# Sliding-window attention: the product of probabilities and reciprocal sums computed on GpSimd instead of the Vector engine

## The chip, the cores and the metric

The kernel runs on one core of a Trainium2 chip. The core's engines are named as the profile names them: PE (TensorE, the matrix products; PEld is its loading of stationary operands), DVE (VectorE), ACT (ScalarE), POOL (GpSimd) and SP (SyncE, which issues most loads). Each runs its own instructions in a fixed order and waits on semaphores for the others. The metric is the device time of one launch in microseconds; before the change it is 1203.77 us, the median of three runs from 1203.2 to 1205.82.

## The reference

A two-layer decoder trunk over 512 tokens of width 1024: an mLSTM layer, then a sliding-window attention layer with sinks, each followed by a layer norm, a squared-ReLU MLP, a second norm and a gated embedding. The change is in the attention of the second layer, where each of 16 heads sees a window of 128 tokens:

```python
scores = jnp.where(valid[None, :, None, None], scores, -jnp.inf)
...
m = jnp.maximum(jnp.max(scores, axis=-1), sink)
e = jnp.exp(scores - m[..., None])
probs = e / (jnp.sum(e, axis=-1) + jnp.exp(sink - m))[..., None]
out = jnp.einsum('bnqkgs,bnskd->bnqkgd', probs.astype(x.dtype), vb).reshape(B, S, D_MODEL)
```

## The kernel before

All products are made in three parts (`mm3`, lines 87 to 90): every float32 operand is split into a rounded high part and the low rest, and PE adds high by high, high by low and low by high. The split costs an ACT copy (the high part) and a DVE subtraction (the low part), for weights in `load_w` (lines 76 and 77) and for every intermediate result.

The attention layer is cut into 16 blocks, named (g, t) here: g is one of four groups of four heads that share a key and value head, t one of four tiles of 128 tokens. `q_group(g, t)` makes the queries of a block (24 products of 256 columns into the bank `mm`, a DVE sum `q` at line 839 that frees the bank, rotation on POOL at lines 786 to 789, transposes, split). `attend(g, t)` does the attention of a block, in this chain:

- PE: eight score products (lines 860 and 861) into two `sc` banks.
- DVE: masked copy (865), maximum (866), then the negative maximum `anm` (871) and the sink term `es` (873).
- ACT: four exponentials (879), which write the probabilities `pr` (128 x 512) and their sums `sm`.
- DVE: sum with the sink (881), reciprocal (882), and the product of `pr` and the reciprocal, spread over 128 columns per head (883).
- PE: four transposes of `pr` (887) into a `pt` bank.
- ACT copies the high part `ah` (891), DVE subtracts for the low part `al` (892).
- POOL, for t > 0: two triangular selects make `bh` and `bl` (899).
- PE: six value products with `ah` and `al`, and six more with `bh` and `bl` (the masked products), at lines 88 to 90 on tiles `pt`. ACT (910) and DVE (911) split the result into `QS`.

The program issues `attend(g, ...)` for four tiles and then `q_group(g + 1, ...)`, so the query products of the next group are the work that covers the chain; in the last group the first products of the output projection (`wo_part`, 128 x 512 into `mm`) take that part. `pr`, `ah`, `al`, `bh` and `bl` have two buffers each, `sc` has three banks, `mm` and `pt` two.

The order in which each engine takes these instructions isn't written by hand. The framework's scheduler sets it when the program is built, from its own estimate of each instruction's duration and engine. So a change of engine for one instruction can move others, on every engine.

## Time and profile before

| what | value |
|---|---|
| median of three runs | 1203.77 us |
| the profiled execution in all | 1205.69 us |
| its span | 1204.0 us |
| granted TensorE clock over the span | 0.998 |
| first and last multiply of line 883 | 674.1 and 761.6 us |

The profile shows one execution. "Busy" is the time in which an engine has an instruction at work, "idle before" the time that it stood still ahead of one, with the instruction that ended the wait. The attention blocks fill about 90 us of the span, from 671 to 761 us; the MLP of the first layer lies before, the output projection, the norm and the second MLP behind. Rows of the timeline give start and duration in us, engine, line, operation, and the tiles written and read.

### The profile page before, as it was taken

To read this page: it belongs to the slowest core of one execution; us is meant where nothing else is said; L and a number is where in the kernel's file an instruction comes from. 1 tells how busy PE (TensorE), PEld (TensorE's weight loads), DVE (VectorE), ACT (ScalarE), POOL (GpSimd) and SP (SyncE) were. 2 spreads that over 40 slices of the span, in tenths; PEclk is the share of its full clock that TensorE was granted. 3 is DMA by queue.
4 is the path that set the end of the run, shared out by engine and by line. 5 is a ranking of instruction groups with operands and counts; after the bars stand their busy time and mean duration, and the time that the engine had idled before them with its cause. 6 is when DMAs were issued, how large, how long until landed. Compare 5 with 4: busy or idle time off the path is not lost. (4 is left out here: it accounts for less than half of the span.)

```text
span 1204.0 us, 15649 instructions
## 1 busy us (share of the span) xinstructions
PE 1178.7 (98%) x5918; PEld 1001.0 (83%) x5918; DVE 879.0 (73%) x1451; ACT 587.5 (49%) x1016; POOL 95.8 (8%) x189
## 2 busy tenths in 40 slices
PE   8999999999999999999999999989999999999998
PEld 7899998888888888888788998779888888888877
DVE  6555556878488589599786888596847848959974
ACT  4645552565464463464344655346645536346431
POOL 1011020100000000001201342110000000000100
PEclk9999999999999999999999999999999999999999
DMA  7322226214505306215252211361350440631511
GB/s 247 101 80 69 84 89 260 90 35 128 153 1 175 105 19 194 68 53 160 76 180 101 71 37 36 122 228 36 94 169 18 140 141 1 191 89 36 155 56 52
DMA packets 35707, 124.54 MB, mean 103 GB/s; under 512 B 4064, under 2 KB 4592, under 8 KB 35632
## 3 DMA queue, kind: packets, MB, share of 16 engines
q1 hardware_dynamic: 33552, 116.46, 30.4%
q0 software_dynamic: 2080, 7.09, 1.8%
q8 instruction: 46, 0.75, 0.2%
q14 instruction: 29, 0.24, 0.1%
HBM read 119.34 MB, written 4.19 MB: 103 GB/s over the span
## 5 line engine op out<-in xcount | busy, mean ns | idle before, releaser
L77 DVE TENSOR_TENSOR wlo<-wraw,whi 128x1024 fp32r<-128x1024 f32 (+1 forms) x168 | 204.1, 1218 | 125.2 <-ACT whi L76 124.2
L76 ACT CAST whi<-wraw 128x1024 fp32r<-128x1024 f32 (+1 forms) x168 | 173.7, 1037 | 239.6 <-PE mm L90 132.8
L88 PE MATMUL mm<-XH,whi 128*128 128x512 f32 (+1 forms) x640 | 235.1, 370 | 1.2 <-ACT ot L230 1.0
L89 PE MATMUL mm<-XL,whi 128*128 128x512 f32 (+1 forms) x640 | 235.9, 369 | 0.0
L90 PE MATMUL mm<-XH,wlo 128*128 128x512 f32 (+1 forms) x640 | 235.7, 369 | 0.0
L88 PE MATMUL mm<-whi,XH 128*128 128x512 f32 (+2 forms) x424 | 146.0, 345 | 3.9 <-DVE q L839 2.2
L89 PE MATMUL mm<-wlo,XH 128*128 128x512 f32 (+2 forms) x424 | 145.3, 343 | 0.0
L90 PE MATMUL mm<-whi,XL 128*128 128x512 f32 (+2 forms) x424 | 144.7, 343 | 0.0
L88 PEld LDWEIGHTS mm<-XH,whi 128*128 128x128 f32 x640 | 120.4, 189 | 21.8 <-ACT ot L230 1.4
L90 PEld LDWEIGHTS mm<-XH,wlo 128*128 128x128 f32 x640 | 121.1, 189 | 20.0
L89 PEld LDWEIGHTS mm<-XL,whi 128*128 128x128 f32 x640 | 121.1, 189 | 19.6
L76 ACT CAST whi<-rb 128x1024 fp32r<-128x1024 f32 x80 | 84.0, 1050 | 101.0 <-PE mm L89 56.4
L77 DVE TENSOR_TENSOR wlo<-rb,whi 128x1024 fp32r<-128x1024 f32 x80 | 97.4, 1221 | 38.9 <-ACT whi L76 38.9
L88 PEld LDWEIGHTS mm<-whi,XH 128*128 128x128 f32 x424 | 79.9, 189 | 13.0 <-DVE q L839 3.9
L89 PEld LDWEIGHTS mm<-wlo,XH 128*128 128x128 f32 x424 | 80.1, 189 | 7.7 <-issue 1.5
L90 PEld LDWEIGHTS mm<-whi,XL 128*128 128x128 f32 x424 | 80.1, 189 | 6.5 <-issue 0.8
L89 PE MATMUL mm<-wlo,S23h 128*128 128x512 f32 x128 | 50.7, 396 | 0.0
L89 PE MATMUL mm<-wlo,S4Ah 128*128 128x512 f32 x128 | 50.6, 395 | 0.0
L88 PE MATMUL mm<-whi,S23h 128*128 128x512 f32 x128 | 50.6, 395 | 0.0
L88 PE MATMUL mm<-whi,S4Ah 128*128 128x512 f32 x128 | 50.6, 395 | 0.0
L90 PE MATMUL mm<-whi,S4Al 128*128 128x512 f32 x128 | 50.3, 395 | 0.0
L633 DVE TENSOR_TENSOR res<-res,mm 128x512 f32<-128x512 f32 x72 | 48.6, 682 | 1.5 <-PE mm L90 1.0
(356 smaller groups left out, 2233.2 us busy)
## 6 DMA issues: line engine op xcount, KB each, us to landing
wraw<-in_w_up_dram SPq DMA_DIRECT2D x64, 512.0 KB, 3.9
rb<-in_w_down_dram SPq DMA_DIRECT2D x48, 512.0 KB, 4.4
wraw<-in_w_down_dram SPq DMA_DIRECT2D x16, 512.0 KB, 3.5
wraw<-in_w_gate_dram SPq DMA_DIRECT2D x16, 512.0 KB, 3.8
wraw<-in_w_vo_dram SPq DMA_DIRECT2D x19, 412.0 KB, 3.5
wraw<-in_w_qk_dram SPq DMA_DIRECT2D x8, 512.0 KB, 3.7
wraw<-in_w_out_dram SPq DMA_DIRECT2D x8, 512.0 KB, 3.9
wraw<-in_w_q_dram SPq DMA_DIRECT2D x8, 512.0 KB, 3.9
```

What stands on the lines that cost most here:

```text
L76: ACT.copy(hi, raw)
L77: eng.tensor_sub(lo, raw, f32(hi))
L88: PE.matmul(o, lh, rh, start=start, stop=False)
L89: PE.matmul(o, lh, rl, start=False, stop=False)
L90: PE.matmul(o, ll, rh, start=False, stop=stop)
L633: V.tensor_add(r[:, h], r[:, h], bank)
```

## The change

Line 883 moves from DVE (`V`) to POOL (`GP`); nothing else is edited.

```diff
         V.tensor_add(sm, sm, es)
         V.reciprocal(sm, sm)
-        V.tensor_mul(pt_, pt_, sm.unsqueeze(3).broadcast_to([P, 2, 2, P]))
+        GP.tensor_mul(pt_, pt_, sm.unsqueeze(3).broadcast_to([P, 2, 2, P]))
         pT = bank("pt")
```

The scheduler gives all four computing engines a new order from the fourth block on. Three places follow.

PE, block (1,1). `pr_6177` is its probabilities, `sc_6272` and `sc_6279` are the scores of block (1,3), `ah_6191` and `al_6192` its own split probabilities. Before, from its transposes on:

```order
L887 MATMUL pt_6186<-ident_66,pr_6177 128x128 x4
L860 MATMUL sc_6279<-KH_5264,QS_5326 128x256
L861 MATMUL sc_6279<-KL_5265,QS_5326 128x256
L860 MATMUL sc_6272<-KH_5264,QS_5326 128x256
L861 MATMUL sc_6272<-KL_5265,QS_5326 128x256
L860 MATMUL sc_6279<-KH_5264,QS_5326 128x256
L861 MATMUL sc_6279<-KL_5265,QS_5326 128x256
L843 MATMUL tp_6361<-ident_66,q_6353 128x128 x2
L88 MATMUL pt_6199<-ah_6191,vo0h_5272 128x256
L89 MATMUL pt_6199<-al_6192,vo0h_5272 128x256
```

After, from the same transposes on:

```order
L887 MATMUL pt_6186<-ident_66,pr_6177 128x128 x4
L860 MATMUL sc_6272<-KH_5264,QS_5326 128x256
L861 MATMUL sc_6272<-KL_5265,QS_5326 128x256
L843 MATMUL tp_6361<-ident_66,q_6353 128x128 x2
L860 MATMUL sc_6279<-KH_5264,QS_5326 128x256
L861 MATMUL sc_6279<-KL_5265,QS_5326 128x256
L860 MATMUL sc_6279<-KH_5264,QS_5326 128x256
L861 MATMUL sc_6279<-KL_5265,QS_5326 128x256
L88 MATMUL mm_6407<-whi_6099,XH_64 128x256
L89 MATMUL mm_6407<-wlo_6100,XH_64 128x256
```

Query products (`mm_6407`, 21 of them before the first value product of the block) now follow where the value products stood.

PE, block (2,2). `ah_6636` and `al_6637` are its split probabilities, `pr_6679` those of the next block, `mm_7021` is a bank of the output projection. Before, behind the last score products that follow its transposes:

```order
L860 MATMUL sc_6906<-KH_5264,QS_5326 128x256
L861 MATMUL sc_6906<-KL_5265,QS_5326 128x256
L88 MATMUL mm_7021<-whi_6875,QS_5326 128x512
L89 MATMUL mm_7021<-wlo_6876,QS_5326 128x512
L90 MATMUL mm_7021<-whi_6875,QS_5326 128x512
L88 MATMUL mm_7021<-whi_6875,QS_5326 128x512
```

After, at the same place:

```order
L860 MATMUL sc_6906<-KH_5264,QS_5326 128x256
L861 MATMUL sc_6906<-KL_5265,QS_5326 128x256
L88 MATMUL pt_6644<-ah_6636,vo1h_5278 128x256
L89 MATMUL pt_6644<-al_6637,vo1h_5278 128x256
L90 MATMUL pt_6644<-ah_6636,vo1l_5279 128x256
L88 MATMUL pt_6644<-ah_6636,vo1h_5278 128x256
L89 MATMUL pt_6644<-al_6637,vo1h_5278 128x256
L90 MATMUL pt_6644<-ah_6636,vo1l_5279 128x256
L88 MATMUL pt_6644<-bh_6640,vs2h_5296 128x256
L887 MATMUL pt_6688<-ident_66,pr_6679 128x128 x4
L88 MATMUL mm_7021<-whi_6875,QS_5326 128x512
```

Fourteen out-projection products stood ahead of the value products; now they stand behind them and behind the next block's transposes.

POOL and DVE, the last four blocks (3,0) to (3,3), whose probabilities are `pr_6918`, `pr_6984`, `pr_7060` and `pr_7117`. `bh_7002` and `bl_7003` belong to (3,1), `bh_7078` and `bl_7079` to (3,2). POOL before:

```order
L899 AFFINE_SELECT bh_6697<-ah_6693 128x512
L899 AFFINE_SELECT bl_6698<-al_6694 128x512
L899 AFFINE_SELECT bh_7002<-ah_6998 128x512
L899 AFFINE_SELECT bl_7003<-al_6999 128x512
L899 AFFINE_SELECT bh_7078<-ah_7074 128x512
L899 AFFINE_SELECT bl_7079<-al_7075 128x512
```

POOL after:

```order
L883 TENSOR_TENSOR pr_6918<-pr_6918,sm_6919 128x512
L883 TENSOR_TENSOR pr_6984<-pr_6984,sm_6985 128x512
L899 AFFINE_SELECT bh_7002<-ah_6998 128x512
L899 AFFINE_SELECT bl_7003<-al_6999 128x512
L883 TENSOR_TENSOR pr_7060<-pr_7060,sm_7061 128x512
L883 TENSOR_TENSOR pr_7117<-pr_7117,sm_7118 128x512
L899 AFFINE_SELECT bh_7078<-ah_7074 128x512
L899 AFFINE_SELECT bl_7079<-al_7075 128x512
```

The multiply of (3,2) stands behind both selects of (3,1), and the selects of (3,2) behind the multiply of (3,3). On DVE at the same place, `al_6933` is the low part of block (3,0), `anm_6979` the negative maximum of (3,1), `sc_7041` a score of (3,2). Before:

```order
L866 TENSOR_REDUCE smax_6964<-sc_6972 128x2
L849 TENSOR_TENSOR QS_5326<-tp_6828,QS_5326 64x2x128
L871 SCALAR_TENSOR_TENSOR anm_6979<-smax_6964,nsink_5270 128x4
L892 TENSOR_TENSOR al_6933<-pt_6927,ah_6932 128x512
L873 TENSOR_TENSOR es_6981<-sinkb_332,anm_6979 128x4
L865 COPY_PREDICATED sc_7041<-mask_328,sc_7041 128x2x128
```

After:

```order
L892 TENSOR_TENSOR al_6933<-pt_6927,ah_6932 128x512
L865 COPY_PREDICATED sc_7041<-mask_328,sc_7041 128x2x128
L849 TENSOR_TENSOR QS_5326<-tp_6867,QS_5326 64x2x128
L871 SCALAR_TENSOR_TENSOR anm_6979<-smax_6964,nsink_5270 128x4
L866 TENSOR_REDUCE smax_7040<-sc_7041 128x2
L873 TENSOR_TENSOR es_6981<-sinkb_332,anm_6979 128x4
```

The low part of (3,0) and a masked copy of (3,2) now stand ahead of the maximum of (3,1).

## Prediction

> **What bounds the kernel now.** I read the page first: busy shares, then the chain that ended last.

> ```profile
> PE 1178.7 (98%) x5918; PEld 1001.0 (83%) x5918; DVE 879.0 (73%) x1451; ACT 587.5 (49%) x1016; POOL 95.8 (8%) x189
> PE 32%; DVE 1%; ACT 0%; issue 0%
> ```

> TensorE sets the end. A change on DVE or GpSimd can only win back time in which PE waits, or add such time. So the second view is busy time by stretch, cut at the attention blocks: 671 to 749 us holds the multiplies of blocks (0,0) to (3,0), 749 to 760 the last blocks that no projection work covers, then the output projection and the first norm.

> ```profile
> core 0: us, PE busy (x) PEld busy (x) DVE busy (x) ACT busy (x) POOL busy (x), PEclk, DMA share, GB/s
> 671.00:749.00 78.00, 74.29 (x570) 69.89 (x569) 66.26 (x177) 44.95 (x173) 27.23 (x65) 1.00 0.14 44
> 749.00:760.00 11.00, 9.32 (x61) 7.59 (x60) 9.91 (x30) 6.34 (x29) 1.27 (x2) 1.00 0.00 0
> 760.00:780.00 20.00, 20.00 (x101) 16.82 (x100) 7.38 (x12) 6.17 (x15) 3.98 (x6) 1.00 0.38 133
> 780.00:812.00 32.00, 28.19 (x159) 23.72 (x158) 30.52 (x45) 13.03 (x19) 5.97 (x4) 1.00 0.67 246
> ```

> PE idles 78.00 - 74.29 = 3.7 us in the covered blocks and 11.00 - 9.32 = 1.7 us in the last ones; from 760 to 780 it does not wait. Hence 5.4 us is the whole prize, and DVE is 85 to 90% busy there. The view of waits says for whom PE waited between 671 and 762:

> ```profile
> PE mm L88 <- DVE q L839: 2.2, 4, 0.7
> PE pt L89 <- DVE al L892: 1.3, 2, 0.9
> PE pt L88 <- DVE QS L911: 0.5, 1, 0.5
> ```

> All three are late DVE work, so the idea has something to win.

> **What the multiply costs on each engine.** DVE and its nearest relatives on GpSimd:

> ```profile
> L883 DVE TENSOR_TENSOR pr<-pr,sm x16: 680/686/1008, 674.1 to 761.6; 128x512 f32<-128x512 f32 x16
> L395 POOL TENSOR_TENSOR ot<-ot,hg 128x1024 f32<-128x1024 f32 x4 | 9.6, 2403 | 44.4 <-ACT ot L394 44.4
> L786 POOL TENSOR_TENSOR ta<-q,cos 128x64 f32<-128x64 f32 x16 | 6.1, 380 | 100.5 <-DVE q L839 89.5 <-DVE es L873 7.5 <-PE pt L90 3.3
> L899 POOL TENSOR_SCALAR_AFFINE_SELECT bh<-ah 128x512 fp32r<-128x512 f32 x12 | 8.1, 676 | 40.6 <-ACT ah L891 40.6
> ```

> Removed: 16 x 0.686 = 11.0 us of DVE. Added: a two-input product of 512 columns on GpSimd, which no row shows. A line through 64 columns (380 ns) and 1024 columns (2403 ns) gives 380 + 448 x 2.11 = 1.32 us; I take that. The ends are 0.68 us (the select of the same tile, one input) and 2.40 us (twice the width). GpSimd gets 16 x 1.32 = 21 us on top of the 28.5 us in the 89 us above: room enough, if the queue's order allows it. [...]

> **Covered blocks, the waits that go.** Block (0,0):

> ```profile
> 673.43 0.18 DVE L882 RECIPROCAL sm<-sm 128x4 f32<-128x4 f32 x1
> ...
> 673.58 0.28 PE L860 MATMUL sc<-KH,QS 128*128 128x256 f32 x1
> ...
> 673.70 0.28 PE L861 MATMUL sc<-KL,QS 128*128 128x256 f32 x1
> ...
> 674.09 0.69 DVE L883 TENSOR_TENSOR pr<-pr,sm 128x512 f32<-128x512 f32 x1
> ...
> 674.82 0.43 DVE L865 COPY_PREDICATED sc<-mask,sc 128x256 f32<-128x256 uint8 x1
> 674.84 0.66 PE L887 MATMUL pt<-ident,pr 128*128 128x128 f32 x4
> ...
> 675.62 0.41 DVE L839 TENSOR_TENSOR q<-mm,bq 128x256 f32<-128x256 f32 x1
> ...
> 676.09 0.39 PE L88 MATMUL mm<-whi,XH 128*128 128x256 f32 x1 [0.59 <-DVE q L839]
> ```

> PE waits 0.59 us for the sum q (it frees the bank), and q stood behind the multiply. Without it the masked copy, whose score (673.70 + 0.28) is done, starts 0.7 us earlier, and q with it. On GpSimd the multiply can start at 673.7, not at 674.09, and ends at 675.0 against 674.78: the transposes slip by 0.2, and after their 0.5 us of issue the product can follow at 675.6 instead of 676.09. I count **-0.5**. So latency is nearly even here: what GpSimd loses in speed it gains by not queueing on DVE.

> ```profile
> 707.49 0.39 PE L89 MATMUL pt<-al,vo0h 128*128 128x256 f32 x1 [0.89 <-DVE al L892]
> ...
> 711.87 0.69 DVE L883 TENSOR_TENSOR pr<-pr,sm 128x512 f32<-128x512 f32 x1
> 712.48 1.22 DVE L77 TENSOR_TENSOR wlo<-wraw,whi 128x1024 fp32r<-128x1024 f32 x1
> 713.73 0.42 DVE L839 TENSOR_TENSOR q<-mm,bq 128x256 f32<-128x256 f32 x1
> ...
> 714.21 0.38 PE L88 MATMUL mm<-whi,XH 128*128 128x256 f32 x1 [0.67 <-DVE q L839]
> 747.62 0.36 PE L88 MATMUL pt<-ah,vo2h 128*128 128x256 f32 x1 [0.53 <-DVE QS L911]
> ```

> Block (1,1) waits 0.89 us for al. In the new PE order 21 projection products, at 0.12 us each (673.58 to 673.70), stand between its transposes and its value products: **-0.9**. At 714.21 q stood behind a multiply and a weight split; now it follows the reciprocal directly: **-0.7**. At 747.62 block (2,3) gets projection products ahead of its value products: **-0.5**. Together **-2.6**.

> **Covered blocks, a wait that comes.** The same reordering takes cover from block (2,2): its value products stood behind 15 short products and 14 of the wide out-projection ones after its transposes; now only the 15 are left, 1.8 us at 0.12.

> ```profile
> 737.41 0.60 PE L887 MATMUL pt<-ident,pr 128*128 128x128 f32 x4
> 739.95 0.68 DVE L892 TENSOR_TENSOR al<-pt,ah 128x512 fp32r<-128x512 f32 x1
> ```

> al was ready 3.2 us after the transposes began; with one multiply less ahead, 2.5 to 2.8; needed some 0.4 + 1.8 = 2.2 after: a wait of about 0.5. The first masked product of that block stands ahead of the next transposes, and its select now queues behind the next block's multiply on GpSimd: 0.6 more. **+1.1**.

> **The last blocks.** Transposes of (3,0), (3,1), (3,2), and the chain between the last two:

> ```profile
> 748.94 0.60 PE L887 MATMUL pt<-ident,pr 128*128 128x128 f32 x4
> ...
> 755.67 0.63 PE L887 MATMUL pt<-ident,pr 128*128 128x128 f32 x4 [0.32 <-DVE es L873]
> ...
> 756.50 0.59 ACT L891 CAST ah<-pt 128x512 fp32r<-128x512 f32 x1
> ...
> 757.25 0.67 DVE L892 TENSOR_TENSOR al<-pt,ah 128x512 fp32r<-128x512 f32 x1
> 757.98 0.64 POOL L899 TENSOR_SCALAR_AFFINE_SELECT bl<-al 128x512 fp32r<-128x512 f32 x1 [0.18 <-DVE al L892]
> 758.15 1.00 DVE L883 TENSOR_TENSOR pr<-pr,sm 128x512 f32<-128x512 f32 x1
> ...
> 759.37 0.60 PE L887 MATMUL pt<-ident,pr 128*128 128x128 f32 x4
> ```

> From (3,2)'s transposes on PE never waits, and the products left are the same number in both orders; so the end moves with 759.37. Select and multiply ran beside each other; in the new GpSimd order the multiply of (3,2) stands behind both selects of (3,1). The chain is then 0.63 + 0.59 + 0.67 + 0.64 + 1.32 and about 0.7 of hand-offs and queueing behind the exponentials = 4.6 us against 759.37 - 755.67 = 3.7: +0.9. Between (3,0) and (3,1) DVE now does al of (3,0) ahead of the maximum of (3,1), and the longer multiply adds to it: +0.5 on 6.7 us. Five masked products of (2,3) that filled that gap (0.6 us) are now ahead of it: +0.6. And the maximum of (3,2), with two inputs in SBUF, meets the running multiply of (3,1). What such a meeting costs:

> ```profile
> 112.27 2.40 POOL L395 TENSOR_TENSOR ot<-ot,hg 128x1024 f32<-128x1024 f32 x1 [10.88 <-ACT ot L394]
> 113.26 2.29 DVE L77 TENSOR_TENSOR wlo<-wraw,whi 128x824 fp32r<-128x824 f32 x1
> L77 DVE TENSOR_TENSOR wlo<-wraw,whi x168: 1016/1224/2289, 21.2 to 1175.2; 128x1024 fp32r<-128x1024 f32 x152, 128x824 fp32r<-128x824 f32 x16
> ```

> The split beside the GpSimd product ended 0.88 us after it: it stood still until GpSimd was done. Here that is 0 to 0.8 us; I take half: +0.4. **Together +2.4.**

> After 780 PE idles 3.8 us behind norms on DVE; the same work, slightly reordered: 0, give or take 0.5.

> **Sum:** -2.6 + 1.1 + 2.4 = **+0.9 us** on the profiled execution (1204.0 span, 1205.69 in all), 1206.6. Its three runs have a median of 1203.77, so I forecast **1204.7**. With the multiply at 0.68 us, (2,2) and the two last steps get 0.64 shorter each: -1.0; at 2.40, 1.08 longer each: +4.1.

> **Rivals.** *Relief wins.* DVE loses 11 us in a stage where it is the late one: all 3.7 us of idle PE up to 749 go, and the last blocks pay only 0.6, one longer multiply: -3.1, 1200.7. For it: all three rows of waits name DVE. Against: the reordering also spends cover, and the last blocks are a chain.

> *GpSimd's multiply becomes the chain (slower).* Place: the transposes of (2,2) to (3,2), which wait for it. Price: at 2.0 us (blocked by a split, or slower than the line) each of (2,2), (3,1), (3,2) adds 0.7, and so does (0,0), whose transposes (674.84) followed DVE's multiply at once: 0.9 + 2.8 = +3.7, 1207.5. It decides from about 1.7 us per multiply. For it: the 2.29 us row, and GpSimd's fixed order. Against: in (0,0) the earlier start pays for most of the longer multiply.

> *The two engines only trade places.* Every DVE op with two SBUF inputs stands still behind the multiply, so DVE gains nothing that PE sees, and the last blocks keep their time because the copy and split there hide it: 0, 1203.8. [...] The 2.29 us row agrees that they meet; whether it eats the gain no row shows yet.

> **How the numbers follow.** Forecast 0.46, relief 0.22, GpSimd chain 0.24, trade 0.08. About 0.2% (2.4 us) is what a measurement of this kernel can tell from no change: faster is below 1201.4, slower above 1206.2. Faster: relief less a little, plus the forecast's low end = 0.23; slower: the GpSimd chain and the forecast's high end = 0.29; same 0.48. The forecast's own range is 1202.5 to 1206.5; both signs hold half the chance, so the range takes in most of both rivals: 1200.5 to 1208.2.

> **What would show it.** GpSimd's multiply at 1.2 to 1.4 us; PE's waits for q near 675 and 714 gone; a new wait of about 1 us around block (2,2); 11 to 13 us from (3,0)'s to (3,2)'s transposes instead of 10.4; PE full for 20 us after. Wrong if the multiply is far from 1.3 us, if PE's idle time up to (3,0) does not fall below 3.7, or if the time differs outside the attention stage.

## The result, and the profile after

| | before | after |
|---|---|---|
| median of 5 runs | 1203.77 us | 1210.36 us |
| lowest to highest | 1203.1 to 1205.82 us | 1209.21 to 1211.33 us |
| the profiled execution: in all, span, mean clock | 1205.69, 1204.0 us, 0.998 | 1210.66, 1209.0 us, 0.996 |

The ratio is 1.0044, interval 1.0033 to 1.0055: the change costs about 5.3 us, with 4.0 to 6.6 us possible. (The two medians are 6.6 us apart, the upper end of this.) The forecast was 1204.7 us, with 1208.2 as its upper end.

First the multiply itself and the waits of the attention stage, 671 to 762 us, after the change (a group's row: count, shortest, median and longest in ns; a wait's row: total, times, longest in us):

```profile
L883 POOL TENSOR_TENSOR pr<-pr,sm x16: 1029/1040/1042, 673.9 to 760.8; 128x512 f32<-128x512 f32 x16
```

```profile
PE mm L88 <- DVE q L839: 1.8, 3, 0.8
PE pt L88 <- DVE al L892: 1.3, 1, 1.3
...
PE pt L887 <- POOL pr L883: 0.4, 1, 0.4
```

GpSimd needs 1.04 us for the product, and TensorE waits for it only once, 0.4 us. The waits for other engines have changed places. The stretches of the prediction, with the same columns, after the change:

```profile
671.00:749.00 78.00, 74.93 (x583) 71.26 (x584) 62.44 (x168) 46.34 (x175) 39.58 (x79) 1.00 0.15 45
749.00:760.00 11.00, 7.44 (x43) 5.55 (x41) 8.09 (x25) 6.23 (x32) 3.23 (x4) 1.00 0.00 1
760.00:780.00 20.00, 19.86 (x102) 16.83 (x103) 6.56 (x10) 5.54 (x10) 4.70 (x8) 1.00 0.32 101
780.00:812.00 32.00, 25.57 (x124) 20.55 (x123) 25.96 (x37) 11.12 (x14) 4.52 (x3) 0.95 0.67 249
```

The covered blocks got better (idle TensorE 3.1 us instead of 3.7), the last blocks worse (3.6 instead of 1.7). Up to the transposes of block (3,2), which start at 760.14 instead of 759.37, that makes +0.8 us (0.2 of it stands there before the stage begins: the same product starts at 670.82 instead of 670.62). The rest comes after 780 us: TensorE idles 32.00 - 25.57 = 6.4 us instead of 3.8, and the granted clock over these 32 us is 0.95 instead of 1.00, which is 1.6 us of full speed. 0.8 + 2.6 + 1.6 = 5.0 us, the difference of the two spans.

What stands there is one stop of TensorE (timeline of the changed kernel, TensorE, then VectorE):

```profile
786.53 0.50 PE L88 MATMUL mm<-whi,QS 128*128 128x512 f32 x1 [4.42 <-DVE res L157]
786.86 0.39 PE L89 MATMUL mm<-wlo,QS 128*128 128x512 f32 x1
787.09 0.49 PE L90 MATMUL mm<-whi,QS 128*128 128x512 f32 x1
787.38 0.63 PE L88 MATMUL mm<-whi,QS 128*128 128x512 f32 x1
787.80 0.63 PE L89 MATMUL mm<-wlo,QS 128*128 128x512 f32 x1
```

```profile
782.29 0.69 DVE L157 TENSOR_TENSOR res<-res,mm 128x512 f32<-128x512 f32 x1 [5.82 <-DMA res<-spill]
...
785.19 1.28 DVE L157 TENSOR_TENSOR res<-res,mm 128x512 f32<-128x512 f32 x2 [1.48 <-DMA res<-spill]
```

The same adds in the kernel before, and the product of TensorE that waited for the second of them:

```profile
779.87 0.69 DVE L157 TENSOR_TENSOR res<-res,mm 128x512 f32<-128x512 f32 x1 [3.71 <-DMA res<-spill]
...
781.20 0.67 DVE L157 TENSOR_TENSOR res<-res,mm 128x512 f32<-128x512 f32 x1
782.45 0.69 DVE L157 TENSOR_TENSOR res<-res,mm 128x512 f32<-128x512 f32 x1 [0.58 <-DMA res<-spill]
```

```profile
781.93 0.50 PE L88 MATMUL mm<-whi,QS 128*128 128x512 f32 x1 [0.57 <-DVE res L157]
```

Behind the attention stage the output projection is added to the residual tiles `res` (line 157), which come back from memory (`spill`, line 946) into space that the attention tiles leave. TensorE goes on 0.06 us after the add of the first tile's second half: before at 781.20 + 0.67, when it waited 0.6 us, after behind 785.19 + 1.28, when it waited 4.4. Two things delay that add. The first reload arrives 2.4 us later. And the scheduler has put the add of the second tile's first half, with its own reload, ahead of it in VectorE's queue. SyncE's issues, before and after:

```profile
771.36 2.91 SPq L83 DMA_DIRECT2D wraw<-in_w_up_dram  x3
774.37 2.09 SPq L946 DMA_DIRECT2D res<-spill  x4
```

```profile
771.95 3.12 SPq L83 DMA_DIRECT2D wraw<-in_w_up_dram  x3
775.17 2.24 SPq L946 DMA_DIRECT2D res<-spill  x4
```

The reloads are issued 0.8 us later, behind three weight loads of 512 KB each for a stage that needs them much later. They wait for nothing of their own: SyncE's longest wait there, 32.2 us before and 33.0 us after, is that of the first of these weight loads, for a buffer that a weight split (line 77) frees. Then the clock (stretches of 2 us, after):

```profile
786.00:788.00 2.00, 1.47 (x5) 1.20 (x6) 2.00 (x4) 0.00 (x0) 0.00 (x0) 0.81 1.04 418
788.00:790.00 2.00, 2.00 (x7) 1.52 (x6) 2.00 (x5) 0.00 (x0) 0.38 (x1) 0.50 1.02 418
```

Soon after TensorE starts again, its clock is halved for 3.4 us (787.25 to 790.66): products start 0.42 us apart (787.38, 787.80), 0.23 before (786.86, 787.09). The stop of 4.42 us stands ahead of it here; in the experiments below the half clock also comes behind less (2.3 us in before_late_reload).

### The profile page after: what moved, and what is told of

It reads as the page before. It is cut to its first block, busy times and chain, and to the rows that moved or that the text cites. A ratio compares the mean times of both kernels' runs of the same rounds, so it can differ in the third digit from the quotient of the medians.

```text
span 1209.0 us, 15663 instructions
## 1 busy us (share of the span) xinstructions
PE 1179.7 (98%) x5918; PEld 1002.3 (83%) x5918; DVE 873.1 (72%) x1435; ACT 587.7 (49%) x1016; POOL 110.8 (9%) x205
## 4 chain that ended last, share of the span: by engine, by line
PE 87%; DVE 6%; ACT 3%; DMA 2%; issue 1%; SPq 0%; POOL 0%; DVEq 0%; ACTq 0%; POOLq 0%
PE mm L88 28%; PE mm L90 28%; PE mm L89 27%; DVE wlo L77 1%; ACT pr L879 1%; PE tp L129 1%; DMA xraw<-in_xT_dram 1%; DMA res<-spill 1%; ACT whi L76 1%; PE tp L88 1%; PE tp L89 1%; PE tp L90 1%; DVE sc L865 1%; DVE QS L849 1%; DVE smax L866 1%
## 5 line engine op out<-in xcount | busy, mean ns | idle before, releaser
L77 DVE TENSOR_TENSOR wlo<-wraw,whi 128x1024 fp32r<-128x1024 f32 (+1 forms) x168 | 205.2, 1224 | 126.9 <-ACT whi L76 126.0
L88 PE MATMUL mm<-XH,whi 128*128 128x512 f32 (+1 forms) x640 | 235.7, 370 | 1.0 <-ACT ot L230 0.8
L90 PE MATMUL mm<-XH,wlo 128*128 128x512 f32 (+1 forms) x640 | 236.1, 369 | 0.0
L89 PE MATMUL mm<-XL,whi 128*128 128x512 f32 (+1 forms) x640 | 236.1, 369 | 0.0
L88 PE MATMUL mm<-whi,XH 128*128 128x512 f32 (+2 forms) x424 | 146.3, 346 | 3.6 <-DVE q L839 1.8
L89 PE MATMUL mm<-wlo,XH 128*128 128x512 f32 (+2 forms) x424 | 145.1, 343 | 0.0
L90 PE MATMUL mm<-whi,XL 128*128 128x512 f32 (+2 forms) x424 | 144.4, 343 | 0.0
L88 PEld LDWEIGHTS mm<-XH,whi 128*128 128x128 f32 x640 | 120.8, 190 | 21.4 <-ACT ot L230 1.2
L90 PEld LDWEIGHTS mm<-XH,wlo 128*128 128x128 f32 x640 | 121.3, 190 | 20.0
L89 PEld LDWEIGHTS mm<-XL,whi 128*128 128x128 f32 x640 | 121.3, 189 | 19.8
L77 DVE TENSOR_TENSOR wlo<-rb,whi 128x1024 fp32r<-128x1024 f32 x80 | 97.6, 1225 | 39.0 <-ACT whi L76 39.0
L88 PEld LDWEIGHTS mm<-whi,XH 128*128 128x128 f32 x424 | 79.9, 189 | 12.6 <-DVE q L839 3.4
L89 PEld LDWEIGHTS mm<-wlo,XH 128*128 128x128 f32 x424 | 80.2, 189 | 7.7 <-issue 1.5
L90 PEld LDWEIGHTS mm<-whi,XL 128*128 128x128 f32 x424 | 80.1, 189 | 6.5 <-issue 0.8
L89 PE MATMUL mm<-wlo,S23h 128*128 128x512 f32 x128 | 50.7, 396 | 0.0
L89 PE MATMUL mm<-wlo,S4Ah 128*128 128x512 f32 x128 | 50.6, 396 | 0.0
L88 PE MATMUL mm<-whi,S23h 128*128 128x512 f32 x128 | 50.6, 395 | 0.0
L88 PE MATMUL mm<-whi,S4Ah 128*128 128x512 f32 x128 | 50.6, 395 | 0.0
L90 PE MATMUL mm<-whi,S4Al 128*128 128x512 f32 x128 | 50.3, 395 | 0.0
```

The source lines that it names most:

```text
L77: eng.tensor_sub(lo, raw, f32(hi))
L88: PE.matmul(o, lh, rh, start=start, stop=False)
L89: PE.matmul(o, lh, rl, start=False, stop=False)
L90: PE.matmul(o, ll, rh, start=False, stop=stop)
```

## The experiments

Three theories were on the table. **A**: the order of the two adds. **B**: the attention stage itself, with the multiply on GpSimd. **C**: the reload that comes late, in whatever order. The kernel before was timed anew beside each group of kernels (medians 1205.03, 1204.97, 1205.00 and 1204.76 us); a ratio of 0.001 is 1.2 us. "First add" is the start of the first add of line 157, "stop" TensorE's wait for these adds, "half clock" whether the stretch behind the stop shows it, all from one profiled execution each, which can lie up to 2.7 us off its kernel's median.

| kernel | median us | ratio and interval | reload issued | first add | stop | half clock |
|---|---|---|---|---|---|---|
| before | 1203.77 | 1 | 774.37 | 779.87 | 0.6 | no |
| after | 1210.36 | 1.0044 (1.0033 to 1.0055) | 775.17 | 782.29 | 4.4 | yes |
| after_adds_as_before | 1208.41 | 1.0032 (1.0020 to 1.0043) | 774.54 | 781.45 | 2.0 | no |
| before_adds_as_after | 1205.71 | 1.0010 (1.0000 to 1.0021) | 773.68 | 779.66 | 2.6 | yes |
| gp_groups_0_2 | 1209.08 | 1.0039 (1.0026 to 1.0051) | 774.16 | 781.23 | 4.9 | yes |
| after_reload_first | 1203.46 | 0.9993 (0.9983 to 1.0002) | 767.05 | 776.09 | none | no |
| before_reload_first | 1201.52 | 0.9970 (0.9958 to 0.9981) | 765.73 | 774.79 | none | no |
| after_bc_behind | 1206.89 | 1.0010 (1.0001 to 1.0019) | 774.87 | 781.88 | 2.7 | yes |
| after_filled_stop | 1206.27 | 1.0014 (1.0005 to 1.0023) | 774.64 | 782.00 | 0.7 | no |
| gp_block_00 | 1204.74 | 0.9995 (0.9986 to 1.0005) | 772.57 | 777.80 | 0.3 | no |
| before_late_reload | 1208.29 | 1.0032 (1.0019 to 1.0046) | 776.13 | 782.36 | 2.3 | yes |
| gp_0_1_reload_first | 1199.64 | 0.9953 (0.9941 to 0.9965) | 764.11 | 773.17 | none | no |
| gp_0_2_reload_first | 1205.08 | 1.0002 (0.9993 to 1.0010) | 769.35 | 778.39 | 0.8 | no |
| gp_groups_0_1 | 1203.37 | 0.9985 (0.9976 to 0.9994) | 771.70 | 777.06 | 0.4 | no |

### after_adds_as_before: the order of the adds put back

```diff
+            if half == 0 and t == 1:
+                late = ps
+                continue
             r = add_res(t, half, ps, None)
+            if half == 1 and t == 0:
+                with tc.issue_after(tc.nc.cur_bb.bb.instructions[-1]):
+                    r1 = add_res(1, 0, late, None)
+                    V.bn_stats(sts[1][:, 0, :], r1)
```

> The changed kernel with the two adds of L157 put back in the old order: the add of (second tile, first half) is queued on VectorE behind the add of (first tile, second half). The attention stage keeps its order. Theory A (the loss is this order: VectorE stands before the second tile's reload, while the add behind it holds the bank that TensorE wants): TensorE's stop at 782 us falls from 4.6 to 1.5-2.2 us, the clock dip behind it goes or shortens, 1205.5-1208. Theory B (the loss is the slower multiply and the later end of the attention stage): nothing changes, 1210. Theory C (the reload itself comes late, whatever stands in which order): the stop stays above 4 us, 1209.5-1210.5.

VectorE's adds in this kernel:

```profile
782.79 0.67 DVE L157 TENSOR_TENSOR res<-res,mm 128x512 f32<-128x512 f32 x1
783.99 0.69 DVE L157 TENSOR_TENSOR res<-res,mm 128x512 f32<-128x512 f32 x1 [0.54 <-DMA res<-spill]
```

The freeing add now needs no second reload. The stop fell to 2.0 us and the half clock behind it went, as A said and C did not, but the time only to 1.0032: 1.4 us won, which the intervals don't tell from nothing, and the 1208.4 us lie above A's range. Two stretches of the changed kernel, then of this one, show where the rest stays:

```profile
780.00:796.00 16.00, 11.59 (x44) 8.97 (x43) 11.85 (x20) 1.04 (x1) 1.65 (x2) 0.89 1.01 394
796.00:812.00 16.00, 13.99 (x82) 11.58 (x81) 14.11 (x18) 10.07 (x13) 2.87 (x2) 1.00 0.33 104
```

```profile
780.00:796.00 16.00, 14.00 (x64) 11.13 (x63) 13.66 (x22) 1.17 (x2) 3.06 (x2) 1.00 0.98 380
796.00:812.00 16.00, 13.70 (x79) 11.93 (x78) 15.45 (x23) 10.33 (x14) 2.91 (x2) 0.89 0.39 132
```

Up to 796 us TensorE works 2.4 us more at full clock; then it waits again, 1.4 us for another add of line 157 and 0.7 us for the layer norm, and the half clock comes there (0.89 of 16 us, 1.8 us). A holds for the stop, not for most of the time.

### before_adds_as_after: the new order in the kernel before

```diff
             if half == 0 and t == 1:
                 r = add_res(t, half, ps, None)
+                second = tc.nc.cur_bb.bb.instructions[-1]
...
             if half == 1 and t == 0:
+                with tc.issue_after(second):
                     r = add_res(t, half, ps, None)
```

> The kernel before, multiply on VectorE, with the two adds of L157 in the order of the changed kernel. A: the first tile's second add now waits for the second reload (which landed by 782.45 us before), TensorE's stop grows from 0.7 to about 2.6 us, 1205.3-1207. B: nothing changes, 1203.8. C: the reload lands as before, so 1203.5-1204.5.

The stop was 2.6 us, as A had it, and the 1205.7 us lie in its range; but the kernel before ran 1205.03 beside it, so the order alone is worth some 1.2 us (1.0010), with an interval that begins at nothing. The profiled execution, 1208.40 us, is one of the longest of this kernel. A may be a part of the loss.

### gp_groups_0_2: the last four blocks back on VectorE

```diff
-        GP.tensor_mul(pt_, pt_, sm.unsqueeze(3).broadcast_to([P, 2, 2, P]))
+        (GP if gi < 3 else V).tensor_mul(pt_, pt_, sm.unsqueeze(3).broadcast_to([P, 2, 2, P]))
```

> GpSimd multiplies in the groups 0 to 2 only; in the last four blocks VectorE does it, as before. The scheduler leaves the adds of L157 in the order of the changed kernel. A: the attention stage ends 0.5-1 us ahead of the kernel before, the stop at 782 us stays at 2-4 us: 1205-1208. B: without the slow last blocks the relief is left alone: 1202.5-1203.5. C: the reload is issued at the old time or sooner, so 1203-1204.5.

No theory had this right: the time hardly moved from that of the changed kernel, and the stop stayed, at 4.9 us. What the last blocks' multiplies cost inside the attention stage is told further below; the kernel's time doesn't show it.

### after_reload_first and before_reload_first: the reload ahead of the next stage's weights

```diff
         nc.sync.dma_start(res[t], spill[t])
+    reload = tc.nc.cur_bb.bb.instructions[-1]
...
-    mlp(1, "left")
+    with tc.issue_after(reload):
+        mlp(1, "left")
```

> The changed kernel with the loads of the next stage's weights (w_up and later) queued on SyncE behind the four reloads of the residual tiles, so that nothing of 512 KB stands ahead of these. A: VectorE need not wait for the second tile, though the adds keep the new order; the stop at 782 us goes below 1 us and with it the clock dip, 1203.5-1206. B: 1210, as the attention stage is untouched. C: as A, 1203.5-1206.

> The kernel before, multiply on VectorE, with the next stage's weight loads queued behind the four reloads, as in after_reload_first (0.9993 of before, 1203.5 us there). Theory C (all of the change's loss beyond the attention stage's 0.3 to 0.8 us is the reload that comes late): this kernel is 0.3-1.5 us under after_reload_first, about 0.9980-0.9990 of before. Theory B (the multiply on GpSimd costs 4 us or more by itself, and the reload's order is a separate gain): it is 4 us or more under after_reload_first, 0.995-0.996 of before.

The changed kernel's adds with the reload first (they keep the new order):

```profile
776.09 0.68 DVE L157 TENSOR_TENSOR res<-res,mm 128x512 f32<-128x512 f32 x1
...
778.62 0.69 DVE L157 TENSOR_TENSOR res<-res,mm 128x512 f32<-128x512 f32 x1 [1.13 <-DMA res<-spill]
```

The first tile is there when the add is due, the stop is gone, and the changed kernel falls by 0.0051 (6.1 us) to the time of the kernel before. But the kernel before gains 3.6 us from the same edit, so the reload's lateness is some 2.5 us of the change's 5.3, a rough figure, as each ratio has an interval of 1.2 us either way. The other 2.8 us (0.9993 against 0.9970) are left with no stop at all: more than C's 0.3 to 1.5, less than B's 4.

### after_bc_behind: the two broadcasts behind the reloads

```diff
-    g, b = bcast(A["mix_ln_g"][1]), bcast(A["mix_ln_b"][1])
+    g, b = bcast(A["mix_ln_g"][1], eng=nc.sync), bcast(A["mix_ln_b"][1], eng=nc.sync)
```

> The changed kernel; the two broadcast loads of the layer norm's g and b (512 KB each) leave GpSimd's queue and stand on SyncE's queue behind the four reloads. Adds of L157 stay in the new order. Theory C2 (the reloads land late because from 779.3 us on the broadcasts take a part of the DMA engines, and a reload issued 0.8 us later falls under them): the first reload lands 6.0 us or less after its issue instead of 7.1, the second about 1.4 us behind it, TensorE's stop falls from 4.6 to 2-3 us, 1.002-1.0035 of before. Theory C1 (the loads of w_up ahead of the reloads alone decide it): landing stays at 7 us, the stop above 4 us, 1.004-1.0045.

```profile
783.21 1.27 DVE L157 TENSOR_TENSOR res<-res,mm 128x512 f32<-128x512 f32 x2
```

The first add still starts 7.0 us after the issue, as C1 said, so the broadcasts don't hold the first reload. The second came sooner: its add now follows with no wait, where it waited 1.48 us. The stop of 2.7 us is as C2 said; the 4.1 us won (1.0044 to 1.0010) are more than it said. With the reload behind the weights, the table has the first add 5.2 to 6.2 us after the issue in the kernels whose groups 2 and 3 are on VectorE, and 6.9 to 7.4 us in those with group 2 on GpSimd. The transfers themselves are slower: in the 8 us from the issue of the first of the three weight loads, the DMA engines moved 283 to 305 GB/s in the first sort (268 in before_late_reload, which holds the reloads back) and 246 to 265 in the second. What makes them slower stays open.

### after_filled_stop: useless products in the stop

```diff
+                if (half, t) == (1, 0):
+                    idle = tp_bank()
+                    with tc.issue_after(last0):
+                        for n in range(16):
+                            PE.matmul(idle, QS[:, 0, tsl(0)], w[3][0][:, 0:512], start=True, stop=True)
```

> The changed kernel with 16 products 128x512 of no use put at the place of TensorE's stop at 782 us (3.7 us at 0.233 us each; their bank is never read), so that TensorE works while it would wait. If the dip of the granted clock to 0.5 behind the stop comes from the stop: the dip goes, the stop's remainder is 0.5-1.2 us, the program gains 1.2-2.5 us, 1.0025-1.0035 of before. If the dip has another cause (the DMA load, the load of VectorE): clock 0.5 stays in the records at 787-790 us, 1.004-1.0045.

The same stretches as above, in this kernel:

```profile
786.00:788.00 2.00, 1.99 (x9) 1.63 (x10) 2.00 (x3) 0.00 (x0) 0.00 (x0) 1.00 1.00 399
788.00:790.00 2.00, 2.00 (x10) 1.65 (x9) 2.00 (x5) 0.00 (x0) 0.91 (x1) 1.00 1.04 420
```

With DMA and VectorE as loaded as before but TensorE busy, the clock stays at 1.00, where it was 0.81 and 0.50. Here the half clock follows from TensorE's own stop. The gain of 3.6 us is more than was expected and more than the 1.6 us of clock; what the rest is was not separated.

### gp_block_00: one block on GpSimd, every other engine's order untouched

```diff
+        (GP if (gi, t) == (0, 0) else V).tensor_mul(pt_, pt_, sm.unsqueeze(3).broadcast_to([P, 2, 2, P]))
```

> The kernel before with the multiply on GpSimd in the first block (0, 0) alone; TensorE's, ScalarE's and SyncE's orders are then those of before. If the multiply on GpSimd does no harm of its own, the wait at 676 us shrinks by about 0.5 us as forecast and the time is 0.999-1.0005 of before. [...]

Transposes of block (0,1) in the kernel before (those of (0,0) start at 674.84), then of (0,0) and (0,1) here:

```profile
680.93 0.60 PE L887 MATMUL pt<-ident,pr 128*128 128x128 f32 x4
```

```profile
673.76 0.66 PE L887 MATMUL pt<-ident,pr 128*128 128x128 f32 x4
...
679.14 0.60 PE L887 MATMUL pt<-ident,pr 128*128 128x128 f32 x4
```

From (0,0) to (0,1) it is 5.38 us instead of 6.09: the wait of 0.59 us for q is gone, and 0.7 us are won where 0.5 were forecast. The time, 0.6 us less, is the same within its interval. In this block the move by itself does no harm.

### before_late_reload: lateness alone

```diff
+    scratch = dpool.tile([1, 64], F32, name="scratch")
+    nc.sync.dma_start(scratch, f32(QS)[0:1, 12, 3 * P:3 * P + 64])
+    with tc.issue_after(tc.nc.cur_bb.bb.instructions[-1]):
         for t in range(NT):
             nc.sync.dma_start(res[t], spill[t])
```

(The adds of line 157 and the loads behind the reloads are held in the old order with the same means.)

> The kernel before, all engines in the order of before, but the four reloads are held on SyncE behind a store of 256 bytes that waits for the last block's output (ScalarE's copy at about 775.3 us), so that they are issued some 1.2-1.5 us later than before (774.37). If lateness is passed on one to one (landing 5.5 us after issue, as before): TensorE's stop grows from 0.7 to 1.7-2.3 us, 1.0005-1.0013 of before. If lateness of this size is enough to explain the changed kernel by itself (landing 7 us after issue, as there): the stop is 3-4 us, with a dip of the clock behind it, 1.002-1.004.

VectorE's first adds, and the stretch behind the stop:

```profile
782.36 1.28 DVE L157 TENSOR_TENSOR res<-res,mm 128x512 f32<-128x512 f32 x2 [6.20 <-DMA res<-spill]
```

```profile
784.00:786.00 2.00, 2.00 (x6) 1.52 (x6) 0.93 (x3) 0.00 (x0) 0.00 (x0) 0.50 1.02 410
```

The issue came 1.76 us late, more than planned, and cost 0.0032, 3.9 us: twice the delay. The time is in the second range, the stop of 2.3 us is not: it is what the delay alone gives (0.6 + 1.7). In the profiled execution the clock is halved twice, behind the stop and again at 807.5 us, some 1.7 us of full speed each, which is enough for the rest. No multiply was moved here, so the 3.9 us are the price of lateness alone.

### gp_0_1_reload_first, gp_0_2_reload_first and gp_groups_0_1: which blocks pay

```diff
+        (GP if gi < 2 else V).tensor_mul(pt_, pt_, sm.unsqueeze(3).broadcast_to([P, 2, 2, P]))
```

(`gi < 3` in the second; the third without the edit of the reload.)

> GpSimd multiplies in the groups 0 and 1 only, VectorE in 2 and 3, and the reloads stand ahead of the next stage's weights. If the relief of the first eight blocks (2 us of TensorE's waits between 660 and 720 us) and the reload's order are gains that add up, and the new waits of 1.4 us at 738 and 1.2 us at 750 us come from the multiplies of group 2 and later: 0.995-0.9965 of before, 0.5-2 us under before_reload_first (0.9970). If the waits come back elsewhere: 0.997-0.999.

> As gp_0_1_reload_first, with group 2 on GpSimd too and only the last four blocks on VectorE. If the new waits at 738 and 750 us come from group 2's multiplies: 1.2-2.5 us above gp_0_1_reload_first, 0.9975-0.9995. If they come from the last blocks: the same as gp_0_1_reload_first within 0.5 us.

> GpSimd multiplies in the groups 0 and 1 only, nothing else touched: the reloads stand behind the loads of w_up as in the kernel before, and the adds of L157 keep the order of before. If the change's own gain is the 1.9 us of waits that go between 660 and 720 us, and its loss begins with group 2: 0.9975-0.9990 of before, TensorE's stop at 780 us 1 us or less. If any use of GpSimd there costs later what it saves: 0.9995-1.002.

With the runs above, the ratios make a table:

| multiplies on GpSimd | reload behind the weights | reload first |
|---|---|---|
| none | 1 | 0.9970 |
| groups 0 and 1 | 0.9985 | 0.9953 |
| groups 0 to 2 | 1.0039 | 1.0002 |
| all | 1.0044 | 0.9993 |

gp_0_1_reload_first and gp_groups_0_1 came out as their first theory said, gp_0_2_reload_first worse than either. Read downwards: groups 0 and 1 win 1.8 and 2.0 us, group 2 costs 6.5 and 5.9, group 3 adds +0.6 and -1.1, which the intervals (some 0.001 each way) don't tell from nothing. Each step holds the multiplies of its blocks and the order that the scheduler makes of them; the two weren't separated. The last blocks in gp_0_1_reload_first and then in gp_0_2_reload_first, whose multiplies there are both on VectorE:

```profile
749.00:754.00 5.00, 4.38 (x27) 3.24 (x25) 4.66 (x16) 3.40 (x18) 0.00 (x0) 1.00 0.00 0
754.00:760.00 6.00, 5.33 (x30) 4.56 (x31) 4.34 (x12) 2.54 (x12) 2.20 (x3) 1.00 0.01 3
```

```profile
749.00:754.00 5.00, 3.39 (x19) 2.61 (x18) 3.98 (x13) 3.04 (x13) 0.00 (x0) 0.93 0.00 2
754.00:760.00 6.00, 4.42 (x21) 3.73 (x20) 4.63 (x16) 2.67 (x13) 1.17 (x2) 0.77 0.00 0
760.00:764.00 4.00, 4.00 (x18) 3.65 (x17) 2.54 (x7) 2.11 (x10) 2.16 (x3) 0.57 0.02 4
```

Group 2's new order leaves 1.9 us more of idle TensorE between 749 and 760 us, and the clock falls twice in the wake of these short waits. (This execution, 1207.52 us, is the longest of its kernel, whose median is 1205.08.) gp_0_1_reload_first is the best version found, 5.7 us under the kernel before (4.2 us or more by its interval).

## Why the prediction was wrong, step by step

**The step that failed** reads "After 780 PE idles 3.8 us behind norms on DVE; the same work, slightly reordered: 0, give or take 0.5." It was +4.2 us: 2.6 of idle time and 1.6 of clock. It took the stage behind the attention as deaf to when the reloads are issued and in which order VectorE adds them. And it read all of the 3.8 us as waits for norms: 0.57 of them, at 781.93, was the wait for the add of a reloaded tile, and it is this wait that grew to 4.42. In before_late_reload a reload issued 1.76 us late cost 3.9 us, twice its delay; before_adds_as_after shows that the order may have a price too (1.0010), after_filled_stop that the stop brings the half clock (0.50 with the stop, 1.00 with the stop filled). The prediction's own last line named this as a way to be wrong, but no chance was given to it.

**The attention stage** was forecast at +0.9 and gave +0.8 at (3,2), in this execution. That it fits so well is in part luck: the last blocks cost 0.7 us less than forecast, and the blocks ahead of them won 0.5 less (at (3,0) 0.95 us, where 1.5 were forecast). By its terms:

- The multiply: 1.32 us forecast from a line through two rows, 1.04 measured.
- (0,0) to (1,3), forecast at -0.5 - 0.9 - 0.7 = -2.1: gp_groups_0_1 gives -1.8 us (interval -2.9 to -0.7). The sum is right. Not every term is: the waits at 676, 707 and 714 us are gone, but in (1,1) a new one for q has come, 0.82 us at 706.23. The fourth gain, -0.5 in block (2,3), belongs to group 2, where the whole is a loss.
- (2,2), forecast at +1.1: the wait is there and of that size, but 0.55 us of it comes from a meeting on VectorE that the term did not have. GpSimd, VectorE and TensorE after the change:

```profile
736.40 1.04 POOL L883 TENSOR_TENSOR pr<-pr,sm 128x512 f32<-128x512 f32 x1 [2.42 <-DVE sm L882]
737.39 1.62 POOL L899 TENSOR_SCALAR_AFFINE_SELECT bh<-ah 128x512 fp32r<-128x512 f32 x1
```

```profile
736.75 1.77 DVE L77 TENSOR_TENSOR wlo<-wraw,whi 128x1024 fp32r<-128x1024 f32 x1 [0.49 <-ACT whi L76]
738.55 0.69 DVE L892 TENSOR_TENSOR al<-pt,ah 128x512 fp32r<-128x512 f32 x1
```

```profile
739.30 0.39 PE L88 MATMUL pt<-ah,vo1h 128*128 128x256 f32 x1 [1.25 <-DVE al L892]
```

The weight split of line 77 takes 1.22 us alone (at 737.52 us in the kernel before); here it met the multiply and took 1.77, `al` stood behind it, and TensorE behind `al`, 1.25 us. The select, in its turn, met the split and took 1.62 instead of 0.64. The rows read as if the later one had stood still until the earlier was done, to within 0.15 us and in both directions: the split ended 1.08 us after the multiply, the select 0.49 us after the split, each a little less than it takes alone. In this profile all six VectorE instructions between 671 and 762 us with both inputs in SBUF that start while a multiply of line 883 runs end behind it: three splits 1.08 to 1.09 us behind, three `anm` 0.02 us. The three sums `q` (line 839, one input in PSUM) that start beside a multiply take 0.41 to 0.42 us, as they do alone.

- The last blocks, forecast at +2.4: (3,0) to (3,2) took 760.14 - 747.99 = 12.15 us instead of 10.43, +1.7. The meeting of `anm` with the running multiply, put at 0 to 0.8, is seen:

```profile
754.04 1.04 POOL L883 TENSOR_TENSOR pr<-pr,sm 128x512 f32<-128x512 f32 x1 [7.63 <-DVE sm L882]
```

```profile
754.28 0.82 DVE L871 SCALAR_TENSOR_TENSOR anm<-smax,nsink 128x4 f32<-128x4 f32 x1
```

A product of four columns (0.16 us in the median of line 871) took 0.82. Next to it, the transposes of (3,1) and (3,2) after the change, then those in gp_groups_0_2, where VectorE multiplies in the last four blocks:

```profile
755.14 0.66 PE L887 MATMUL pt<-ident,pr 128*128 128x128 f32 x4 [0.43 <-POOL pr L883]
...
760.14 0.66 PE L887 MATMUL pt<-ident,pr 128*128 128x128 f32 x4
```

```profile
754.98 0.60 PE L887 MATMUL pt<-ident,pr 128*128 128x128 f32 x4
...
758.58 0.60 PE L887 MATMUL pt<-ident,pr 128*128 128x128 f32 x4
```

From (3,1) to (3,2) it is 5.0 us, against 3.7 before: the +1.3 that the prediction had for the chain and the meeting (though with a multiply of 1.04 us its working gives only 1.0). With the multiplies back on VectorE it is 3.6, so this part is theirs, or their order's. From (3,0) to (3,1) it is 7.15 us instead of 6.73: +0.4 where the other two terms had 1.1, so these were too large. The kernel's time doesn't show the 1.3 us: gp_groups_0_2 won nothing that can be measured.

**The rivals.** "Relief wins" came true for groups 0 and 1 alone, at -1.8 instead of -3.1. "GpSimd's multiply becomes the chain" had the right sign for the wrong reason: it needed 1.7 us per multiply, and TensorE waits 0.4 us for GpSimd in all. "Trade places" is refuted by gp_groups_0_1, though the meetings it rests on are real.

What no term held is the clock: in the profiled executions of six of the seven kernels that have group 2 on GpSimd, the mean granted clock between 749 and 760 us is 0.84 to 0.86, in no other kernel below 1.00. The changed kernel's own is the seventh, with 1.00: its idle time there is no shorter, but fell otherwise on the clock's stretches of 3.41 us (last section).

## What to carry to other kernels

Follow a stage's end to what is issued behind it: here a delay of 1.76 us in a reload's issue became 3.9 us of the kernel's time. Where a tile is needed at once, its load belongs ahead of any prefetch in the same queue: that edit alone was worth 3.6 us. And when an operation moves to GpSimd, move it only in those blocks whose waits the profile names, since the scheduler's new order can cost others more than it wins: groups 0 and 1 won 1.8 us here, group 2 cost 6.5, by its multiplies or by the order.

## What was not expected of the hardware

```profile
799.56:802.97 3.41, 1.91 (x17) 1.61 (x15) 3.41 (x5) 2.09 (x4) 0.00 (x0) 1.00 0.64 199
798.60:802.01 3.41, 1.50 (x11) 1.33 (x12) 3.41 (x5) 2.47 (x3) 0.00 (x0) 1.00 0.72 273
802.01:805.42 3.41, 3.41 (x18) 3.41 (x17) 3.41 (x7) 1.54 (x2) 0.00 (x0) 0.50 0.69 179
```

A stop of 2.0 us passed without it (after_adds_as_before): 0.5 us of it lay in one stretch, 1.5 in the next.
- A first reload of 512 KB let its add start 5.2 (gp_block_00) to 7.4 us (after_filled_stop) after its issue with three loads ahead of it; kernels whose issues on SyncE look alike differ by some 1.5 us, and the cause stays open.
